# First projection weights split early, triangular inverses from two eight-row halves, one routing of all 1024 tokens

## The chip, the cores and the metric

The kernel runs on one core of a Trainium2 chip. The metric is the device time of one execution in microseconds (us). The core has five engines that work side by side from programs of their own: PE (TensorE, matrix products), DVE (VectorE), ACT (ScalarE), POOL (GpSimd) and SP (SyncE, which here only issues transfers). Each engine takes its instructions strictly in order; semaphores make it wait for other engines and for DMA transfers. SP and ACT each have a DMA queue of their own.

## The reference

1024 tokens of width 1024 in fp32 pass a first block (input projection, multiscale pool, RWKV7 mixing, output projection, LayerNorm, mixture of experts, LayerNorm) and then a second block of two attention layers with modulations from a conditioning vector. What the change touches is in the first block:

```python
def rwkv7_step(state, inp):
    r, decay, k, v, kk, a = inp
    sa = jnp.einsum('bhij,bhj->bhi', state, -kk)
    state = (state * decay[:, :, None, :]
             + sa[..., None] * (kk * a)[:, :, None, :]
             + v[..., None] * k[:, :, None, :])
    out = jnp.einsum('bhij,bhj->bhi', state, r)
...
    g_prob = jax.nn.softmax(hf @ router_group + router_group_b, axis=-1)
    g_top_p, g_idx = lax.top_k(g_prob, 1)
    e_sel = jnp.take_along_axis(e_logits, g_idx[:, :, None], axis=1)[:, 0]
    e_top_logit, e_idx = lax.top_k(e_sel, TOP_K)
    weights = g_top_p * jax.nn.softmax(e_top_logit, axis=-1)
...
    hid = jax.nn.silu(xb @ exp_gate[e]) * (xb @ exp_up[e])
    return (hid @ exp_down[e]) * wgt[:, None]
```

The scan over tokens is computed in chunks of 64: the steps of a chunk become products with the inverse of a unit lower triangular 64 x 64 matrix. The modulations ("mods") of the second block are 48 small products of the conditioning vector with 1024 x 128 weight blocks.

## The kernel before, in words

fp32 accuracy comes from splitting each operand into a high and a low fp32r part and adding three products (`mm3`, lines 104 to 106: hi·hi, lo·hi, hi·lo). A weight block is loaded (512 KB), its high part is copied by ACT (`wh`, line 460), and its low part is subtracted by POOL (`wl`, line 467).

Five stages follow each other in the trace: `phase_lowrank` (0 to 111 us), `phase_units` (to about 825), `phase_out` (to 939), `phase_moe` (to about 1260), the second block (to the end, untouched by the change).

- `phase_lowrank` projects the columns of the low-rank branches and makes decay and gates. A `Timeline` sets its order. Its tile pools are freed at its end, and the tiles of `phase_units` take that memory. Twelve memsets on POOL (lines 430 to 443) clear them, after the last transfers out of the old tiles.
- `phase_units` works on 12 units (6 head pairs x 2 halves of the sequence). The lanes of a unit (project, tokens, within, solve, inverse, chain, finish and so on) are generators; the table `PLAN` says at which slot each advances, relative to the unit's slot 24·v, and `ORDER` ranks lanes within a slot. So several units overlap, with a unit each 24 slots or some 48 us. `project` multiplies by three weight blocks j = 0, 1, 2 of 24 matmuls each, issues the load of a block two ahead, and splits the next one. The load is one of SP's, into a single buffer `w`.
- `solve` inverts, for 64 matrices at once (8 chunks x 2 heads x 4 diagonal blocks, one per partition), a 16 x 16 triangle, row by row on DVE: 15 steps of a product and a reduction. Then the result `Tn` goes out to DRAM (`tnd`) and comes back in eight loads to the block layout `T16`; `inverse` transposes it on DVE into `T16T` (line 745) and widens it to 64 x 64 by products.
- `chain` carries the state through the chunks of a unit. PE, ACT (`XB` and `R`, line 786) and DVE (`XA` and `R`, lines 784 and 807) hand each step on to one another.
- `mods` is a generator too; `MODP` gives the slots of its 96 pieces. A piece has eight matmuls (line 1723) on a 512 KB load from ACT's queue, then a copy on ACT, two selecting matmuls (line 1730) and a sum on DVE. After the 24th and 48th a transpose of the collected gates follows on PE (line 1741).
- `phase_out` makes the output projection, LayerNorm and router logits of the token tiles; `Route.part` picks groups and experts for tiles 0 to 3 in the middle and for 4 to 7 at the end, `slots` turns ranks into row numbers by products with one-hot matrices, and the expert weights are already loaded and partly split ("presplit", line 1431 on POOL). Then `phase_moe` gathers the tokens of each expert (indirect transfers from POOL) and runs 32 experts.

The 15 steps of `solve` before (lines 717 to 722) read:

```python
for t in range(1, 16):
    nc.vector.tensor_tensor(pr[:, :t, :t], Tn[:, 0:t, 0:t].rearrange("p s c -> p c s"),
                            LT[:, 0:t, t:t + 1].rearrange("p s o -> p o s").to_broadcast([64, t, t]), op=OP.mult)
    nc.vector.tensor_reduce(Tn[:, t, 0:t], pr[:, :t, :t], axis=AX.X, op=OP.add)
    yield
```

Of the kernel before, what the change touches and what calls it, by code (L numbers as in the profile page):

```python
# [129 lines left out]
def phase_mix(g):  # L130

    nc, tc, a = g.nc, g.tc, g.a
    c = ExitStack()
    with c:
        big = c.enter_context(tc.tile_pool(name="mxx", bufs=1, reuse_waits="tile"))
        xh, xl = (big.tile([P, KT, 512], F32R, name=n) for n in ("xh", "xl"))
        g.csil = big.tile([P, KT, 32], F32, name="csil")  # L140
        phase_lowrank(g, xh, xl)
        phase_units(g, [xh[:, k] for k in range(KT)], [xl[:, k] for k in range(KT)])


def phase_lowrank(g, xh0, xl0):

    nc, tc, a = g.nc, g.tc, g.a
    with ExitStack() as c:
        pool = lambda n, b, **k: c.enter_context(tc.tile_pool(name=n, bufs=b, reuse_waits="tile", **k))
        big, wp, zp, one = pool("pjx", 1), pool("pjw", 2), pool("pjy", 2), pool("pj1", 1)  # L150
# [47 lines left out]
        def w_load(col0):  # L198
            W[col0] = wp.tile([P, KT, P], F32, name="w")
# [171 lines left out]
XSTEP, PSTEP, PSTEP2, BOFF, BSTEP = 2.0, 0.9, 1.4, 8, 2.39  # L371
PAR1, PREP1 = 17.55, 18.1
# [12 lines left out]
    "solve": [-22, -22, -22, -22, -22, -20, -20, -20, -20, -20, -20, -19, -18, -18, -17, -17],  # L385
# [15 lines left out]
MODP = [-69] + [p + i for p in sorted([24 * u + d for u in range(-3, 8) for d in (8, 12, 17)] + [24 * u + 3 for u in range(-2, 9)]  # L401
                                     + [-27, -3, 21, 45]) for i in range(2)]
# [9 lines left out]
def phase_units(g, xh, xl):  # L412
    nc, tc, a = g.nc, g.tc, g.a
    with ExitStack() as c:
        wp = c.enter_context(tc.tile_pool(name="uw", bufs=2, reuse_waits="tile"))
# [28 lines left out]
        f = sm.tile([P, NU, HC], F32, name="f")  # L444
        mk = cv(g, "maskL").rearrange("p (o x t) -> p o x t", o=1, x=2)
        U = [Ctx() for _ in range(NU)]
        W = {}

        def wload(b):
            if b < 3 * NU:  # L450
                v, j = divmod(b, 3)
                col0 = 256 + (6 * j + v % NPAIR) * P
                W[b] = wp.tile([P, KT, P], F32, name="w" if b else "wm", bufs=1)
                nc.sync.dma_start(W[b], a["w_in"][0, :, col0:col0 + P].rearrange("(k p) c -> p k c", p=P))

        def wsplit(b):
            if b < 3 * NU:
                w = W[b]
                wh, wl = (wp.tile([P, KT, P], F32R, name=n) for n in ("wh", "wl"))
                nc.scalar.activation(wh, w, AF.Copy)  # L460
                W[b] = (wh, wl, w)

        def wsplit2(b):
            if b < 3 * NU:
                wh, wl, w = W[b]
                for c0 in range(0, KT, 2):
                    nc.gpsimd.tensor_tensor(wl[:, c0:c0 + 2], w[:, c0:c0 + 2], wh[:, c0:c0 + 2].bitcast(F32), op=OP.subtract)  # L467
# [93 lines left out]
        def tokens(v):  # L561
# [34 lines left out]
            fv = f[:, v, :, None]  # L596
# [116 lines left out]
        def solve(v):  # L713

            u = U[v]
            pr = sm.tile([64, 15, 15], F32, name="pr")
            LT = u.LT
            for t in range(1, 16):
                nc.vector.tensor_tensor(pr[:, :t, :t], Tn[:, 0:t, 0:t].rearrange("p s c -> p c s"),
                                        LT[:, 0:t, t:t + 1].rearrange("p s o -> p o s").to_broadcast([64, t, t]), op=OP.mult)  # L720
                nc.vector.tensor_reduce(Tn[:, t, 0:t], pr[:, :t, :t], axis=AX.X, op=OP.add)
                yield
            nc.sync.dma_start(g.tnd[v % 2], Tn.rearrange("p a b -> p (a b)"))
            d = g.tnd[v % 2]
            for hd in range(2):
                for b in range(4):
                    o = 64 * hd + 16 * b
# [282 lines left out]
def phase_out(g, hres, ex, early):  # L1010

    nc, tc, a = g.nc, g.tc, g.a
    with ExitStack() as c:
# [210 lines left out]
        for _ in r4:  # L1224
            pass
# [1916 lines left out]
```

## Time and profile before

| what | value |
|---|---|
| runs | 3299.97, 3303.45, 3313.67 us (median 3303.45) |
| profiled execution | 3299.23 us, span 3297.5 us |
| mean granted TensorE clock | 0.947 of full speed |
| PE busy | 2958.0 us (90%) |
| DVE busy | 2053.0 us (62%) |
| ACT busy | 1587.1 us (48%) |
| POOL busy | 1705.2 us (52%) |
| PE weight loads (beside the matmuls) | 2085.7 us (63%) |

The span runs from the first to the last instruction; the execution's own time adds 1.7 us around it. PE is the busiest engine, so the time is PE's work plus the gaps in it. A gap's releaser is the event that ended it. What an engine other than PE does matters where it ends such a gap.

### The profile page before, as it was taken

To read this page: it belongs to the slowest core of one execution; us is meant where nothing else is said; L and a number is where in the kernel's file an instruction comes from. 1 tells how busy PE (TensorE), PEld (TensorE's weight loads), DVE (VectorE), ACT (ScalarE), POOL (GpSimd) and SP (SyncE) were. 2 spreads that over 40 slices of the span, in tenths; PEclk is the share of its full clock that TensorE was granted. 3 is DMA by queue.
4 is the path that set the end of the run, shared out by engine and by line. 5 is a ranking of instruction groups with operands and counts; after the bars stand their busy time and mean duration, and the time that the engine had idled before them with its cause. 6 is when DMAs were issued, how large, how long until landed. Compare 5 with 4: busy or idle time off the path is not lost. (4 is left out here: it accounts for less than half of the span.)

```text
span 3297.5 us, 49255 instructions
## 1 busy us (share of the span) xinstructions
PE 2958.0 (90%) x17406; PEld 2085.7 (63%) x17406; DVE 2053.0 (62%) x3309; ACT 1587.1 (48%) x3058; POOL 1705.2 (52%) x1916
## 2 busy tenths in 40 slices
PE   7789899888779986899988898988998989999998
PEld 5466666656557655799845454467776756565556
DVE  2167677763679877775256675747257246666656
ACT  4345555553459876432144444545345235554442
POOL 0266667665435453643046565767356216464665
PEclk9789999988879998899999999999999989999999
DMA  5476776554889997423121111246134311111136
GB/s 201 148 180 164 197 179 154 146 159 132 274 280 320 325 333 249 144 81 107 57 65 49 45 50 39 79 145 224 37 103 154 112 49 63 47 45 39 45 107 219
DMA packets 430972, 457.26 MB, mean 139 GB/s; under 512 B 123336, under 2 KB 351171, under 8 KB 430595
## 3 DMA queue, kind: packets, MB, share of 16 engines
q1 hardware_dynamic: 366944, 400.95, 39.5%
q10 hardware_dynamic: 56162, 36.04, 3.6%
q0 software_dynamic: 7616, 17.09, 1.6%
q8 instruction: 138, 2.26, 0.3%
q14 instruction: 112, 0.91, 0.1%
HBM read 329.39 MB, written 101.11 MB: 131 GB/s over the span
## 5 line engine op out<-in xcount | busy, mean ns | idle before, releaser
L2107 ACT ACTIVATE p<-st 128x512 f32<-128x512 f32 (+1 forms) x672 | 377.7, 585 | 378.6 <-PE st L2105 309.1
L2026 DVE TENSOR_REDUCE mx<-s 128x1 f32<-128x1280 f32 x256 | 380.6, 1487 | 273.0 <-PE s L2025 273.0
L2119 POOL TENSOR_TENSOR acc<-acc,p 128x256 f32<-128x256 f32 x512 | 414.9, 842 | 70.6 <-ACT p L2107 69.2
L2128 PE MATMUL o<-p,V 128*64 128x512 f32 (+1 forms) x1344 | 319.8, 597 | 0.0
L1431 DVE TENSOR_TENSOR wl<-wr,wh 128x1024 fp32r<-128x1024 f32 x156 | 228.1, 1490 | 41.6 <-ACT wh L1430 41.5
L2119 DVE TENSOR_TENSOR acc<-acc,p 128x512 f32<-128x512 f32 x256 | 228.3, 892 | 13.6 <-ACT p L2107 6.7
L104 PE MATMUL pz<-xh,wh 128*128 128x512 f32 x440 | 219.7, 499 | 2.1 <-ACT wh L460 2.1
L1430 ACT ACTIVATE wh<-wr 128x1024 fp32r<-128x1024 f32 x192 | 198.9, 1055 | 40.2 <-DMA wr<-in_exp_up_dram 19.4
L106 PE MATMUL pz<-xh,wl 128*128 128x512 f32 x440 | 180.1, 409 | 15.0 <-POOL wl L467 13.6
L105 PE MATMUL pz<-xl,wh 128*128 128x512 f32 x440 | 180.7, 411 | 0.0
L2144 POOL TENSOR_TENSOR rg<-rg,gt 128x256 f32<-128x256 f32 x72 | 64.5, 895 | 214.7 <-ACT rg L2141 213.5
L2119 POOL TENSOR_TENSOR acc<-p 128x256 f32<-128x256 f32 x72 | 53.6, 762 | 227.9 <-ACT p L2107 223.7
L2128 PEld LDWEIGHTS o<-p,V 128*64 128x64 f32 x1344 | 82.0, 136 | 140.4 <-issue 136.3
L104 PE MATMUL pj<-hh,wh 128*128 128x512 f32 (+1 forms) x416 | 160.8, 387 | 9.2 <-DVE xk L2782 4.6
L1789 POOL TENSOR_TENSOR wl<-wr,wh 128x512 fp32r<-128x512 f32 (+1 forms) x70 | 88.5, 1276 | 151.9 <-ACT wh L1787 151.6
L1431 POOL TENSOR_TENSOR wl<-wr,wh 128x1024 fp32r<-128x1024 f32 x36 | 89.1, 2477 | 146.5 <-ACT wh L1430 131.0
L106 PE MATMUL pj<-hh,wl 128*128 128x512 f32 (+1 forms) x416 | 156.4, 376 | 0.5 <-POOL wl L1789 0.5
L105 PE MATMUL pj<-hl,wh 128*128 128x512 f32 (+1 forms) x416 | 156.2, 376 | 0.0
L2105 PE MATMUL st<-QQ,K 128*128 128x512 f32 (+1 forms) x352 | 149.9, 427 | 4.5 <-ACT p L2107 4.3
L467 POOL TENSOR_TENSOR wl<-w,wh 128x256 fp32r<-128x256 f32 x140 | 110.5, 820 | 78.2 <-ACT wh L460 64.6
L106 PE MATMUL pj<-wh,hl 128*128 128x256 f32 x480 | 141.1, 294 | 4.6 <-POOL hl L1870 4.5
L105 PE MATMUL pj<-wl,hh 128*128 128x256 f32 x480 | 140.4, 293 | 4.7 <-DVE wl L1789 4.7
(524 smaller groups left out, 8457.4 us busy)
## 6 DMA issues: line engine op xcount, KB each, us to landing
wr<-in_exp_gate_dram SPq DMA_DIRECT2D x64, 512.0 KB
wr<-in_exp_up_dram SPq DMA_DIRECT2D x64, 512.0 KB
wr<-in_exp_down_dram SPq DMA_DIRECT2D x32, 1024.0 KB
w<-in_l_w_out_dram SPq DMA_DIRECT2D x56, 512.0 KB
wm<-in_l_w_mod_dram ACTq DMA_DIRECT2D x48, 512.0 KB
w<-in_w_in_dram SPq DMA_DIRECT2D x39, 512.0 KB
wr<-in_l_w_in_dram SPq DMA_DIRECT2D x33, 512.0 KB
y<-ysd SPq DMA_DIRECT2D x16, 512.0 KB
```

The source lines that it names most:

```text
L104: nc.tensor.matmul(out, lh, rh, start=start, stop=False)
L105: nc.tensor.matmul(out, lh, rl, start=False, stop=False)
L106: nc.tensor.matmul(out, ll, rh, start=False, stop=stop)
L467: nc.gpsimd.tensor_tensor(wl[:, c0:c0 + 2], w[:, c0:c0 + 2], wh[:, c0:c0 + 2].bitcast(F32), op=OP.subtract)
L1430: nc.scalar.activation(wh, w, AF.Copy)
L1431: eng.tensor_tensor(wl, w, wh.bitcast(F32), op=OP.subtract)
L1789: eng.tensor_tensor(st["l"][:, ks], st["w"][:, ks], st["h"][:, ks].bitcast(F32), op=OP.subtract)
L2026: nc.vector.tensor_reduce(m[:, j:j + 1], ps.rearrange("p a b -> p (a b)")[:, :SK], axis=AX.X, op=OP.max)
L2105: nc.tensor.matmul(st[:, :n], kk[:, kt * P:(kt + 1) * P], qv[:, pt.q0:pt.q0 + n], start=(j == 0), stop=(j == len(passes) - 1))
L2107: nc.scalar.activation(p[:, :n], st[:, :n], AF.Exp, scale=self.scale)
L2119: (nc.gpsimd if e == 1 else nc.vector).tensor_tensor(a, r.p[r.kts[0], e][:, cs] if r.first else a, r.p[r.kts[i], e][:, cs], op=OP.add)
L2128: nc.tensor.matmul(pt.po[64 * e:64 * e + 64, :n], pt.out["V"](e, kt), r.p[kt, e][:, :n], start=(r.first and i == 0), stop=(r.last and i == ...
```

## The change

Four parts. (1) The functions that load and split the unit projection's weights move into a class whose pool is opened ahead of `phase_lowrank`; block 0 is loaded and split and block 1 loaded inside `phase_lowrank` (`FIRSTW`), and the weight tiles no longer lie in memory that this stage frees. (2) `MODP` puts six fewer mods ahead of slot 0 and five instead of four into each of the units 0 to 7; the transposes after mods 24 and 48 come with the next piece. (3) `solve` inverts both 8 x 8 diagonal halves of each 16 x 16 triangle in the same 7 steps, and makes the lower left quarter from two products of 512 elements with their reductions. ACT copies a transposed `Tn` into `LT`, a second DRAM tile `ttd` and eight more loads fill `T16T`, and the two DVE transposes per unit go. (4) All eight token tiles are routed at once at the end of `phase_out`; the five presplit pieces on POOL go, and five pieces come to DVE at the end of the routing and after the first gather.

```diff
+        w = Weights(g, wp)
+        phase_lowrank(g, xh, xl, wp, w)
+        phase_units(g, [xh[:, k] for k in range(KT)], [xl[:, k] for k in range(KT)], wp, w)
...
+        for dt, f, b in FIRSTW:
+            at(ts[3] + dt, f, first, b)
...
+FIRSTW = (-12, Weights.load, 0), (4, Weights.load, 1), (8, Weights.split, 0), (10, Weights.split2, 0)
...
-    "solve": [-22, -22, -22, -22, -22, -20, -20, -20, -20, -20, -20, -19, -18, -18, -17, -17],
+    "solve": [-22, -21, -21, -20, -20, -19, -19, -18, -18, -17, -16],
...
-MODP = [-69] + [p + i for p in sorted([24 * u + d for u in range(-3, 8) for d in (8, 12, 17)] + [24 * u + 3 for u in range(-2, 9)]
-                                     + [-27, -3, 21, 45]) for i in range(2)]
+MODP = [-69] + [p + i for p in [-64, -55, -45, -36, -27, -16, -7] + [24 * u + d for u in range(8) for d in (3, 8, 12, 17, 21)] + [195]
+                for i in range(2)]
...
-            for t in range(1, 16):
...
+            for t in range(1, 8):
+
+                x = pr[:, 0:2, 0:t, 0:t]
+                nc.vector.tensor_tensor(x, h8(Tn, [[B, 2], [1, t], [16, t]]),
+                                        h8(LT[:, 0:1, t:t + 1], [[B, 2], [0, t], [16, t]]), op=OP.mult)
+                nc.vector.tensor_reduce(h8(Tn[:, t:t + 1, 0:1], [[B, 2], [1, t]]), x, axis=AX.X, op=OP.add)
                 yield
...
+            nc.vector.tensor_tensor(pr, h8(LT[:, 0:1, 8:9], [[1, 8], [0, 8], [16, 8]]),
+                                    h8(Tn, [[0, 8], [1, 8], [16, 8]]), op=OP.mult)
+            yield
+            nc.vector.tensor_reduce(m8, pr, axis=AX.X, op=OP.add)
+            yield
+            nc.vector.tensor_tensor(pr, h8(Tn[:, 8:9, 8:9], [[16, 8], [0, 8], [1, 8]]),
+                                    h8(m8, [[0, 8], [1, 8], [8, 8]]), op=OP.mult)
+            yield
+            nc.vector.tensor_reduce(Tn[:, 8:16, 0:8], pr, axis=AX.X, op=OP.add)
+            nc.scalar.activation(Tt, Tn.rearrange("p t c -> p c t"), AF.Copy)
+            for x, T, d in ((0, Tn, g.tnd[v % 2]), (1, Tt, g.ttd[v % 2])):
+                nc.sync.dma_start(d, T.rearrange("p a b -> p (a b)"))
+            for x, d in ((0, g.tnd[v % 2]), (1, g.ttd[v % 2])):
+                for hd in range(2):
+                    for b in range(4):
+                        o = 64 * hd + 16 * b
+                        dst = T16T[o:o + 16, :, hd, 16 * b:16 * b + 16] if x else T16[o:o + 16, :, 16 * b:16 * b + 16]
+                        nc.sync.dma_start(dst, bass.AP(
+                            tensor=d.tensor, offset=d.offset + (2 * b + hd) * 2048, ap=[[16, 16], [256, 8], [1, 16]]))
...
-            for e, sl in enumerate((lo, hi)):
-                nc.vector.transpose(T16T[sl, :, e, :], T16[sl])
...
-    "presplit": [40.1, 40.15, 40.2, 40.25, 43.6],
...
-    "route": [37, 38, 39, 40, 41, 42, 43, 44, 45],
...
+        def route():
+
             pr = pt.tile([P, 512], F32, name="pr")
+            for i, _ in enumerate(rt.part(0, 8, pr[:, 0:256].rearrange("p (i e) -> p i e", e=NE))):
+                if i == 4:
+                    shift(7, v, 0, 2)
+                    nc.scalar.dma_start(g.hd[7 * P:8 * P, :], hres[7])
+            slots(g, rt.rp, pr[:CAP, 256:320])
+            slot_rows(g, g.idx.rearrange("p q e -> p (q e)"), pr[:CAP, 256:320])
+            for _ in range(3):
+                ex.next(v, 0)
...
-        for _ in route(4, 8):
-            pass
+        route()
...
+        yield
         if n == 23:
...
-        yield
```

Where instructions move, three places matter. First PE at the end of `phase_lowrank`. `pz` is the accumulator of j = 0 (832 before, 829 now), `wh` and `wl` its weights; the rows of `zl`, `lw` and `lg` are the stage's own last products. Before:

```order
L284 MATMUL pA_725<-lg_135,gu_133 128x512
L104 MATMUL pz_832<-xh_107,wh_825 128x512
L105 MATMUL pz_832<-xl_108,wh_825 128x512
L335 MATMUL pA_730<-zl_721,pw1_213 128x512
L284 MATMUL pA_761<-lg_135,gu_133 128x512
L106 MATMUL pz_832<-xh_107,wl_826 128x512
L104 MATMUL pz_832<-xh_107,wh_825 128x512
```

Now (865 is the accumulator of j = 1):

```order
L313 MATMUL pA_738<-lg_137,gu_135 128x512
L104 MATMUL pz_829<-xh_109,wh_629 128x512
L105 MATMUL pz_829<-xl_110,wh_629 128x512
L106 MATMUL pz_829<-xh_109,wl_630 128x512
L104 MATMUL pz_865<-xh_109,wh_842 128x512
L105 MATMUL pz_865<-xl_110,wh_842 128x512
L364 MATMUL pA_743<-zl_734,pw1_215 128x512
L313 MATMUL pA_774<-lg_137,gu_135 128x512
L106 MATMUL pz_865<-xh_109,wl_843 128x512
```

All 24 products of j = 0 now stand ahead of the stage's last eight, and what stands behind those is j = 1.

Second, POOL at the same place: the subtraction for block 0 and the memsets. `T`, `L`, `H`, `Tn`, `Sc` are tiles of `phase_units`. Before:

```order
L430 MEMSET T_796 128x512
L435 MEMSET L_798 128x1024
L440 MEMSET Tn 64x16
L443 MEMSET Sc 128x384
L467 TENSOR_TENSOR wl<-wm,wh 128x256 x4
L467 TENSOR_TENSOR wl<-w,wh 128x256 x12
```

Now:

```order
L171 TENSOR_TENSOR wl<-wm,wh 128x256 x4
L461 MEMSET T_805 128x512
L466 MEMSET L_807 128x1024
L471 MEMSET Tn 64x16
L474 MEMSET Sc 128x384
L171 TENSOR_TENSOR wl<-w,wh 128x256 x12
```

Block 0's four subtractions pass the memsets; those of block 1 stay behind them.

Third, SP's queue around the load of a weight block that follows a solve (`T_796` and `T_805` are `T16`; `XA`, `XB` belong to the chain, `mix` to the unit's output). Before:

```order
L454 DMA w<-in_w_in_dram 128x8x128
L705 DMA XA<-vt 64x4x64 x4
L705 DMA XB<-vt 64x4x64 x4
L723 DMA tnd_96<-Tn 64x256
L728 DMA T_796<-tnd_96 16x8x16 x8
L454 DMA w<-in_w_in_dram 128x8x128
```

Now:

```order
L158 DMA w<-in_w_in_dram 128x8x128
L716 DMA XA<-vt 64x4x64 x4
L716 DMA XB<-vt 64x4x64 x4
L753 DMA tnd_97<-Tn 64x256
L753 DMA ttd_99<-LT 64x256
L759 DMA T_805<-tnd_97 16x8x16 x8
L759 DMA T16T<-ttd_99 16x8x16 x8
L158 DMA w<-in_w_in_dram 128x8x128
```

A write and eight loads more stand ahead of the same weight load.

## Rows read from the trace of the kernel before

**Rows 1.** The windows view by stage. Columns: start:end, us, busy us (instructions) per engine, PEclk, DMA share, GB/s.

```profile
111.00:155.00 44.00, 26.59 (x129) 20.16 (x130) 2.31 (x8) 6.93 (x12) 19.39 (x29) 0.69 0.40 128
...
235.00:825.00 590.00, 535.06 (x5522) 377.13 (x5522) 412.62 (x1106) 303.73 (x676) 382.79 (x537) 0.95 0.62 162
...
939.00:1260.00 321.00, 301.95 (x1452) 208.10 (x1451) 275.18 (x312) 259.10 (x347) 164.94 (x93) 0.98 1.02 327
```

**Rows 2.** The timeline of PE, 94 to 235. Columns: start us, busy us, instruction, [idle before <-releaser].

```profile
103.17 3.37 PE L335 MATMUL pA<-zl,pw 128*128 128x512 f32 x4 [4.30 <-issue]
...
124.33 0.80 PE L106 MATMUL pz<-xh,wl 128*128 128x512 f32 x1 [13.57 <-POOL wl L467]
...
147.53 1.08 PE L1723 MATMUL pA<-wm,csil 128*32 128x128 f32 x16 [1.53 <-DMA wm<-in_l_w_mod_dram]
...
155.78 0.66 PE L575 MATMUL pA<-const,z 128*128 128x128 f32 x4 [0.19 <-DVE z L526]
...
214.83 2.76 PE L652 MATMUL pA<-G,BK 64*128 64x128 f32 x16 [5.10 <-DVE BK L619]
```

**Rows 3.** The timeline of POOL, 110 to 150, same columns.

```profile
116.11 1.84 POOL L435 MEMSET L<- 128x1024 f32 x2 [2.32 <-DMA gtp<-gt]
...
123.56 2.77 POOL L467 TENSOR_TENSOR wl<-wm,wh 128x256 fp32r<-128x256 f32 x4
```

**Rows 4.** The timeline of ACT's DMA queue, 95 to 150, same columns.

```profile
143.68 0.37 ACTq L1710 DMA_DIRECT2D wm<-in_l_w_mod_dram  x1
```

**Rows 5.** The waits of PE from 235 to 780: us in total, times, longest us.

```profile
PE cA L793 <- DVE XA L807: 17.4, 27, 4.9
...
PE pA L1741 <- DVE gcol L1735: 5.6, 2, 2.8
...
PE cB L805 <- ACT XB L786: 5.3, 6, 2.4
```

**Rows 6.** The lines of DVE from 160 to 780: busy us, mean ns | idle before, releaser.

```profile
L719 DVE TENSOR_TENSOR pr<-Tn,LT 64x1 f32<-64x1 f32 (+4 forms) x180 | 88.1, 489 | 11.4 <-DMA LT<-labd 7.2
...
L721 DVE TENSOR_REDUCE Tn<-pr 64x1 f32<-64x1 f32 (+4 forms) x180 | 41.6, 231 | 6.2
...
L745 DVE STREAM_TRANSPOSE T16T<-T 64x512 f32<-64x512 f32 x24 | 16.9, 705 | 0.4
...
L771 DVE TENSOR_TENSOR T<-pA,T32T 64x512 f32<-64x512 f32 x22 | 15.0, 683 | 1.1 <-PE pA L750 0.7
```

**Rows 7.** The timeline of SP's DMA queue, 496 to 520, columns as in rows 2.

```profile
500.51 0.49 SPq L723 DMA_DIRECT2D tnd<-Tn  x1
...
504.40 3.65 SPq L728 DMA_DIRECT2D T<-tnd  x8
...
508.46 0.39 SPq L454 DMA_DIRECT2D w<-in_w_in_dram  x1
```

**Rows 8.** The timelines of ACT and, last row, PE at two weight splits.

```profile
403.02 1.06 ACT L460 ACTIVATE wh<-w 128x1024 fp32r<-128x1024 f32 x1 [1.39 <-DMA w<-in_w_in_dram]
...
514.63 1.06 ACT L460 ACTIVATE wh<-w 128x1024 fp32r<-128x1024 f32 x1 [0.26 <-DMA w<-in_w_in_dram]
...
404.37 0.27 PE L805 MATMUL cB<-XB,TK 128*64 128x64 f32 x1 [2.43 <-ACT XB L786]
```

**Rows 9.** The timelines of PE (first three) and DVE at the routing, 900 to 950.

```profile
912.24 1.89 PE L1140 MATMUL pl<-rw,ht 128*128 128x36 f32 x8 [11.76 <-DVE lgt L1146]
...
933.12 0.44 PE L1294 MATMUL pr<-both,trir 128*128 128x128 f32 x1 [6.92 <-DVE both L1287]
...
944.10 1.51 PE L1490 MATMUL pt<-const,xg 96*128 96x96 f32 x8 [3.97 <-DMA xg<-hd,idx]
...
902.37 2.29 DVE L1277 TENSOR_TENSOR t<-t,sel 128x32 f32<-128x32 f32 x1
...
930.70 0.19 DVE L1277 TENSOR_TENSOR t<-t,sel 128x32 f32<-128x32 f32 x1
```

**Rows 10.** The waits of ACT from 1120 to 1260, columns as in rows 5.

```profile
ACT wh L1430 <- DMA wr<-in_exp_up_dram: 18.0, 11, 3.6
```

More of the change, by code (lines that the diff above doesn't have):

```diff
@@ L139, in phase_mix, with __init__, load, split @@
         xh, xl = (big.tile([P, KT, 512], F32R, name=n) for n in ("xh", "xl"))
[L140 to L145, printed above, removed]
+        g.csil = big.tile([P, KT + 16, 2], F32, name="csil")
+        wp = c.enter_context(tc.tile_pool(name="uw", bufs=2, reuse_waits="tile"))
+        w = Weights(g, wp)
+        phase_lowrank(g, xh, xl, wp, w)
+        phase_units(g, [xh[:, k] for k in range(KT)], [xl[:, k] for k in range(KT)], wp, w)
+class Weights:
+    def __init__(self, g, wp):
+        self.g, self.wp, self.W = g, wp, {}
+    def load(self, b):
+        if b < 3 * NU:
+            v, j = divmod(b, 3)
+            col0 = 256 + (6 * j + v % NPAIR) * P
+            self.W[b] = self.wp.tile([P, KT, P], F32, name="w" if b else "wm", bufs=1)
+            self.g.nc.sync.dma_start(self.W[b], self.g.a["w_in"][0, :, col0:col0 + P].rearrange("(k p) c -> p k c", p=P))
+    def split(self, b):
+        if b < 3 * NU:
+            w = self.W[b]
+            wh, wl = (self.wp.tile([P, KT, P], F32R, name=n) for n in ("wh", "wl"))
+            self.g.nc.scalar.activation(wh, w, AF.Copy)
+            self.W[b] = (wh, wl, w)
+    def split2(self, b):
+        if b < 3 * NU:
+            wh, wl, w = self.W[b]
+            for c0 in range(0, KT, 2):
+                self.g.nc.gpsimd.tensor_tensor(wl[:, c0:c0 + 2], w[:, c0:c0 + 2], wh[:, c0:c0 + 2].bitcast(F32), op=OP.subtract)
+def phase_lowrank(g, xh0, xl0, wp, first):
     nc, tc, a = g.nc, g.tc, g.a
@@ L443, in phase_units @@
         nc.gpsimd.memset(Sc, 0.0)
-        f = sm.tile([P, NU, HC], F32, name="f")
         mk = cv(g, "maskL").rearrange("p (o x t) -> p o x t", o=1, x=2)
         U = [Ctx() for _ in range(NU)]
[L447 to L467, printed above, removed]
+        W, wload, wsplit, wsplit2 = weights.W, weights.load, weights.split, weights.split2
         O = {}
@@ L1205, in phase_out @@
             at(t, early)
-        r4 = route(0, 4)
-        for t in OUT["route"]:
-            at(t, lambda: next(r4, None))
         at(40, lambda: (cw.close(), ex.open()))
@@ L1212, in phase_out @@
                       (0.4, lambda: turn(7, 0)), (0.5, lambda: turn(7, 1)), (0.6, lambda: keep(7, 0)), (0.7, lambda: keep(7, 1)),
[L1213 to L1215 removed]
+                      (0.8, lambda: gain(7, e, 0, 2)), (0.9, lambda: logits(7, 0)), (1.0, lambda: logits(7, 1)),
+                      (1.4, lambda: logit_b(7))):
             at(t + dt, f)
[L1217 to L1218 removed]
         for t in OUT["again"]:
@@ L1321, in weights, with slots, slot_rows @@
         v.tensor_tensor(g.w12[:, 1], g.w12[:, 0], d, op=OP.mult)
-def slots(g, pool, pt, i0, i1, name="slotA"):
+def slots(g, pool, pt, name="slotA", bufs=2):
     nc = g.nc
-    A = pool.tile([P, 2, i1 - i0, CAP], F32R, name=name)
     for j in range(2):
-        nc.vector.tensor_tensor(A[:, j], cv(g, "iota")[:, None, :CAP].to_broadcast([P, i1 - i0, CAP]),
-                                g.rank[:, j, i0:i1, None].to_broadcast([P, i1 - i0, CAP]), op=OP.is_equal)
-    yield
-    for i in range(i0, i1):
-        for j in range(2):
-            nc.tensor.matmul(pt, A[:, j, i - i0], g.tokv[:, j, i].rearrange("p q e -> p (q e)"), start=(i == i0 and j == 0), stop=(i == i1 - 1 and j == 1))
-def slot_rows(g, idx, pt, rows, first):
-    if first:
-        return g.nc.vector.tensor_scalar(rows, pt, 2048.0, None, op0=OP.add)
-    else:
-        return g.nc.vector.tensor_tensor(idx.rearrange("p q e -> p (q e)"), pt, rows, op=OP.add)
+        for i0 in (0, 4):
+            A = pool.tile([P, 4, CAP], F32R, name=name, bufs=bufs)
+            nc.vector.tensor_tensor(A, cv(g, "iota")[:, None, :CAP].to_broadcast([P, 4, CAP]),
+                                    g.rank[:, j, i0:i0 + 4, None].to_broadcast([P, 4, CAP]), op=OP.is_equal)
+            for i in range(4):
+                nc.tensor.matmul(pt, A[:, i], g.tokv[:, j, i0 + i].rearrange("p q e -> p (q e)"),
+                                 start=(j + i0 + i == 0), stop=(j == 1 and i0 + i == 7))
+def slot_rows(g, rows, pt):
+    return g.nc.vector.tensor_scalar(rows, pt, 2048.0, None, op0=OP.add)
 DE = 256
```

73 lines of the change are left out of this document (25 added, 48 removed).

## The prediction, as it went on record

> **What bounds the kernel now.** I read the busy shares of the page first, then the windows by stage, then in each stage that the change touches the timeline of PE with the idle time ahead of each instruction, and last the queues of the engines that end those gaps. PE is busy 90% of the span, and in the unit stage 535 of 590 us [rows 1]: whatever is taken off another engine counts only as far as that engine ends a gap of PE.
>
> Four places hold such gaps. At the start of the units PE is busy 26.6 of 44 us, at a granted clock of 0.69 [rows 1]: it stands 13.57 us for a weight's low part from POOL, and POOL made it at 123.56, as soon as its memsets were through, which in turn waited for transfers out of the old tiles [rows 2, 3]. Through the units DVE ends the largest group of gaps, 17.4 us in 27 waits, beside 5.6 us in two waits of a transpose for the sum just ahead of it [rows 5]. ACT ends 5.3 us [rows 5]. At the routing PE waits 11.76 us for logits that DVE adds behind a routing whose operations on 32 elements last 2.29 us, where the same operation lasts 0.19 us later [rows 9]. In the experts' stage the transfers are full all the time (share 1.02, 327 GB/s), and late in it ACT waits 18.0 us for arriving weights [rows 1, 10].
>
> **The start of the units (12 us gained).** Block 0 is split ahead of the memsets, and all 24 products of j = 0 stand ahead of the low-rank stage's last products. There PE idled 4.30 us [rows 2]; 22 products more at the window's mean of 26.59/129 = 0.21 us are 4.5 us, so they fit into that idle. The 13.57 us stay: j = 1 now waits for the same memsets and for the subtraction behind them, in the very place where j = 0 stood. What is gained is the time of one of three blocks. They fill, with three mods, the stretch from 124.33 to 155.78 [rows 2]: a third of 31.5 us is 10.5. Six mods leave the stage before slot 0. Their products return one per later unit and so gain nothing, but a mod at the start comes before its load has landed (1.53 us of idle at 147.53 [rows 2], 3.85 us after the issue at 143.68 [rows 4]); I count that once: 10.5 + 1.5 = 12. Upper bound: that wait for all six, 10.5 + 9.2 = 19.7. Lower bound: 2, if the chain of unit 0 sets the pace, since PE there waited 5.10 us for DVE's `BK` [rows 2].
>
> **The two transposes after the mods (5 us).** They now come with the next piece, when the sum has long been made. 5.6 us [rows 5] go; each transpose may meet another small wait, so I take 5, between 0 and 5.6.
>
> **The inverse (6 us).** Before, a unit costs DVE (88.1 + 41.6 + 16.9)/12 = 12.2 us [rows 6]. After, 7 steps of a product and a reduction at 0.49 + 0.23 make 5.0 us; two products and two reductions of 512 elements at the 0.68 us of line 771 [rows 6] make 2.7, in all 7.8. The reduction of 512 has no row of its own; that of line 721 lies below it and the product is the nearest of that size. So DVE saves 4.4 us per unit and 53 us in all. This is not PE's time. Of PE's 17.4 us of waiting behind line 807 [rows 5] I give back a third, 6: the rest follows the chain's own round trip, whose sums wait for PE. Bounds 0 and 17.4. ACT's new copy of 64 x 256 is smaller than the weight copy of 1.06 us [rows 8], so at most 1 us per unit; ACT is busy 304 of 590 us [rows 1], which hides it unless the last reduction is late: behind the copy, in ACT's order, stand the chain's `XB` and `R`.
>
> **The transfers of the inverse (11 us lost).** SP issues in order. Before, `tnd` goes out at 500.51, the eight loads at 504.40 for 3.65 us, then at 508.46 the weight load [rows 7], whose data ACT splits at 514.63 after having waited 0.26 us for them [rows 8]: so that load is just in time. Now a write and eight more loads stand ahead of it. At 3.65 us for eight, the weight load leaves 3.65 us later; where the last reduction, which moves behind `G` and one slot back, also delays the first write, up to 1.65 us more, 5.3 in all. Landing took 514.37 - 508.46 = 5.9 us with another 512 KB block on the way from ACT's queue; one block alone took 3.85 us [rows 4], and 3.65 us later that other block is through. So the data come 3.65 + 3.85 - 5.9 = 1.6 us late by the one price and 5.3 us late by the sum of the others. ACT stands meanwhile, and behind its split stand the chain's copies. That this reaches PE, the trace shows at 403.02: ACT waited 1.39 us for such a load, and PE then 2.43 us for `XB` [rows 8]. Nine solves have a weight load behind them; at the first two the chain isn't running yet. 7 x 1.6 = 11. Bounds 0 (the next gap of ACT takes it) and 9 x 5.3 = 48.
>
> The Trainium skill (DMA: Bandwidth & Descriptors, "Rules for kernel authors") advises to join small transfers, because below 64 KB one pays mostly overhead, and gives about 2.0 us fixed per transfer under "Anatomy of one DMA"; that speaks against eight more loads of 8 KB. Paid one after the other that would be an estimated 16 us ahead of each weight load, and the sum would come out slower by a hundred. The trace differs for SP's queue: eight were issued in 3.65 us, 0.46 us each [rows 7], so the fixed part overlaps, and I use the row.
>
> **The routing (4 us).** The first half's routing leaves the middle, and with it PE's 11.76 us wait for the logits [rows 9]. The routing at the end handles eight tiles instead of four: some twenty operations that grow by a third of 0.19 us [rows 9], an estimate of 1.3 us. The first gathered tokens would reach PE, instead of at 944.10 [rows 9], 10.5 us earlier. But expert weights move at 327 GB/s all through the next stage [rows 1], and ACT waits for them later [rows 10]. The five early split pieces on POOL freed load buffers; without them I count 12 instead of 14 loads of 1 MB begun before the first gather, and two loads at 1.05 MB / 327 GB/s = 3.2 us give 6.4 back. 10.5 - 6.4 = 4. Bounds -6 (nothing gained, all given back) and 11.8.
>
> **The sum.** 12 + 5 + 6 + 4 - 11 = 16 us less than the profiled execution's 3299.23: 3283. The median of the runs is 4.2 us above that execution, the fastest run 0.7 above; I keep near the execution and say **3284**.
>
> **Rivals.**
> - *The weight load takes back more than all the rest (slower).* Place: SP's queue behind `T16T`, then ACT's split, then PE's chain. If every one of the nine loads comes 5.3 us late, 48 us go; the relief of DVE is then worth nothing, since ACT ends the gaps, and 12 + 5 + 4 = 21 remain: 27 slower, 3326. It decides from about 4.2 us of PE per load: 9 x 4.2 = 38 is 17 more than the 21 that remain. For: 0.26 us of slack, and 1.39 us turned into 2.43 [rows 8]. Against: the load lands faster alone [rows 4], and a queue that is late may still find a later, slower unit. Chance 0.18.
> - *The start gives nothing.* The round trip of unit 0 through DVE, POOL and ACT replaces the memsets, as at 214.83 [rows 2]: 2 instead of 12, so 3293. For: PE's work before slot 0 thins out by six mods. Against: PE is busy nearly without a break from 155.78 to that wait, so it has had work to move up. Chance 0.15.
> - *The routing's gain is lost to the transfers.* If the experts' stage is bound by its loads from end to end, an earlier start gains nothing and the two loads cost 6.4: 3283 + 10 = 3293. For: share 1.02 [rows 1]. Against: loads waited for are 18.0 us late in the stage [rows 10], while PE is busy 302 of 321 us [rows 1]. Chance 0.12.
> - *The change doesn't free DVE where it ends gaps.* Then 6 us less, 3289, inside the forecast's own spread.
>
> **How the numbers follow.** A measurement of this kernel can tell about 0.5%, 16.5 us, from no change: faster is below 3287, slower above 3320. The forecast has 0.55, of which 0.47 lie below 3287 and 0.08 above, as its sum stands only 3 us from that bound. With 0.15 and 0.12 for the two rivals at 3293, no change has 0.35; slower has 0.18. The terms' spreads upward of the gain are 8, 11, 8 and, for the weight loads, 11 us, together some 20 to 24: low end **3260**. The other end goes to **3320**: it takes in both rivals at 3293 and a weight load that costs 37 us more than I take, and leaves out the worst of the first rival.
>
> **What would show it.** In the changed profile PE should run the whole of j = 0 before 111 us and still wait some 13 us for `wl`, and unit 0's transposes should start near 144 instead of 155.78. No wait for `gcol` should be left. DVE's time per inverse should be near 7.8 us. In ACT's waits, the one for `w` in the unit stage should grow from a few us to some 15; if it grows to 40 and PE's wait for `XB` with it, the first rival holds. PE's first product on gathered tokens should stand some 10 us less after the last unit than now, and ACT's waits for expert weights grow. I am wrong if `w` costs nothing (then the time is near 3272) or if the start's gap only moves to another releaser.

## The result, and the profile after

The changed kernel took 3337.95 us, the median of 8 runs from 3327.39 to 3347.64, against 3306.93 for the kernel before: a ratio of 1.0073, 95% interval 1.0052 to 1.0094. It is slower by 0.7%, where 3284 and a range up to 3320 were forecast. The profiled execution took 3329.10 us, its span 3327.3 us.

The windows by stage, against [rows 1], with the same columns:

```profile
111.00:155.00 44.00, 29.42 (x147) 22.23 (x148) 4.23 (x10) 12.88 (x19) 20.82 (x31) 0.77 0.38 114
...
235.00:825.00 590.00, 509.75 (x5261) 361.66 (x5261) 348.31 (x887) 286.26 (x638) 358.62 (x494) 0.89 0.64 159
...
939.00:1260.00 321.00, 291.37 (x1384) 202.53 (x1385) 271.18 (x336) 245.76 (x328) 158.05 (x89) 0.94 1.00 323
```

At the start the same 44 us hold more PE work. In the unit stage the same 590 us hold less: 5261 matmul records instead of 5522, at a mean granted clock of 0.89 instead of 0.95. The timeline of PE, against [rows 2, 9] (rows of the units' start, of the routing and of the first gathered tokens):

```profile
122.76 0.80 PE L106 MATMUL pz<-xh,wl 128*128 128x512 f32 x1 [14.03 <-POOL wl L171]
...
144.81 0.60 PE L585 MATMUL pA<-const,z 128*128 128x128 f32 x4
...
953.18 0.55 PE L1306 MATMUL pr<-both,trir 128*128 128x256 f32 x1 [7.04 <-DVE both L1304]
...
965.97 1.52 PE L1504 MATMUL pt<-const,xg 96*128 96x96 f32 x8 [3.70 <-DMA xg<-hd,idx]
```

The wait for the low part is still there (14.03 us), and unit 0's transposes start at 144.81 instead of 155.78. The transposes of the next two units start at 178.65 and 222.45, where they stood at 191.62 and 235.82: 13.0 and 13.4 us earlier. From then on the lead melts. The sixth and tenth units' transposes start at 384.35 and 609.63, against 380.68 and 577.35, and the last state of the chain is written at 854.38 instead of 816.60. So between the third unit and the end of the chain 51 us are lost. After that the changed kernel is faster again: from the last state to the first gathered tokens it takes 111.6 us instead of 127.5, and from there to the last expert's output 333.0 instead of 326.8 (1298.98 - 965.97, and 1270.86 - 944.10). The second block takes the same time in both, within 2 us.

What PE waits for from 220 to 790, against [rows 5]:

```profile
PE cB L833 <- ACT XB L814: 38.8, 19, 5.1
...
PE cA L821 <- DVE XA L835: 1.0, 2, 0.6
...
PE pA L1757 <- DVE gcol L1750: 0.3, 1, 0.3
```

The wait behind DVE's state update (line 835, line 807 before) has gone from 17.4 to 1.0 us, and the wait for `gcol` from 5.6 to 0.3. In their place PE waits 38.8 us for ACT's chain copy `XB`, where it was 5.3. What ACT waits for from 140 to 800:

```profile
ACT wh L164 <- DMA w<-in_w_in_dram: 41.4, 13, 4.8
...
ACT LT L751 <- DVE Tn L750: 30.0, 11, 3.2
```

These two stand ahead of the chain copies in ACT's order. Before, in the same stretch:

```profile
ACT wh L460 <- DMA w<-in_w_in_dram: 3.3, 5, 1.4
```

One unit shows how it comes about. SP's queue, against [rows 7]:

```profile
520.01 0.49 SPq L753 DMA_DIRECT2D tnd<-Tn  x1
520.68 0.49 SPq L753 DMA_DIRECT2D ttd<-LT  x1
523.40 3.66 SPq L759 DMA_DIRECT2D T<-tnd  x8
527.17 4.61 SPq L759 DMA_DIRECT2D T16T<-ttd  x8
531.87 0.40 SPq L158 DMA_DIRECT2D w<-in_w_in_dram  x1
```

From the write of `tnd` to the issue of the weight load pass 11.86 us, where it was 7.95. On the mean of the nine solves with a weight load behind them these are 12.1 us (10.8 to 13.5) and 7.0 (5.8 to 8.0). ACT in the same unit, against [rows 8], at the transposing copy and at the weight split:

```profile
520.02 0.64 ACT L751 ACTIVATE LT<-Tn 64x256 f32<-64x256 f32 x1 [3.22 <-DVE Tn L750]
...
535.94 1.06 ACT L164 ACTIVATE wh<-w 128x1024 fp32r<-128x1024 f32 x1 [3.40 <-DMA w<-in_w_in_dram]
```

And PE's next product of the chain:

```profile
537.29 0.37 PE L833 MATMUL cB<-XB,TK 128*64 128x64 f32 x1 [2.78 <-ACT XB L814]
```

ACT came to the split at 532.54 and stood 3.40 us; PE stood 2.78 us for `XB`, which ACT makes right behind the split. What the granted clock did around this stall, in windows of 4 us, with the columns of [rows 1]:

```profile
532.00:536.00 4.00, 2.51 (x31) 1.48 (x30) 1.18 (x3) 0.57 (x3) 3.02 (x4) 1.00 0.72 203
536.00:540.00 4.00, 2.71 (x42) 2.18 (x42) 0.52 (x2) 2.06 (x5) 2.78 (x4) 0.61 0.73 225
540.00:544.00 4.00, 4.00 (x20) 2.91 (x18) 0.65 (x3) 0.69 (x3) 0.62 (x1) 0.50 0.75 196
544.00:548.00 4.00, 4.00 (x56) 3.30 (x59) 2.11 (x6) 0.44 (x2) 0.00 (x0) 0.61 0.64 125
```

PE is busy for 5.2 of the 8 us from 532 to 540, and then works on at a granted clock of 0.50, the lower of its two levels (1.2 GHz), from 540 to 544, and at 0.61 on the mean of the four microseconds on either side.

What the inverse costs PE over all units can be read beside the fourth run below, the changed kernel with the inverse of before. The windows reach from the transposes of the first unit to those of the twelfth, first the changed kernel, then that run, with the columns of [rows 1]:

```profile
144.81:714.28 569.47, 496.61 (x5013) 357.39 (x5011) 335.50 (x830) 281.06 (x598) 348.59 (x469) 0.90 0.65 158
```

```profile
142.79:679.03 536.24, 480.62 (x5013) 344.27 (x5013) 375.57 (x971) 274.65 (x588) 345.20 (x470) 0.96 0.67 165
```

Both hold 5013 matmul records. Of the 33.2 us between them 16.0 are busy time, the same products at a lower granted clock (0.90 instead of 0.96), and 17.2 are idle time of PE.

### The profile page after: what moved, and what is told of

Same layout as the page of the kernel before. It is cut to its first block, busy times and chain, and to the rows that moved or that the text cites. A ratio compares the mean times of both kernels' runs of the same rounds, so it can differ in the third digit from the quotient of the medians.

```text
span 3327.3 us, 49266 instructions
## 1 busy us (share of the span) xinstructions
PE 2979.2 (90%) x17402; PEld 2101.9 (63%) x17402; DVE 1996.1 (60%) x3111; ACT 1596.5 (48%) x3070; POOL 1705.0 (51%) x1912
## 5 line engine op out<-in xcount | busy, mean ns | idle before, releaser
L1445 DVE TENSOR_TENSOR wl<-wr,wh 128x1024 fp32r<-128x1024 f32 x161 | 235.4, 1488 | 42.4 <-ACT wh L1444 42.3
L171 POOL TENSOR_TENSOR wl<-w,wh 128x256 fp32r<-128x256 f32 x140 | 111.6, 828 | 87.7 <-ACT wh L164 84.0
L1445 POOL TENSOR_TENSOR wl<-wr,wh 128x1024 fp32r<-128x1024 f32 x31 | 77.1, 2487 | 138.9 <-ACT wh L1444 98.6
```

The costliest lines, as they stand in the source:

```text
L171: self.g.nc.gpsimd.tensor_tensor(wl[:, c0:c0 + 2], w[:, c0:c0 + 2], wh[:, c0:c0 + 2].bitcast(F32), op=OP.subtract)
L1445: eng.tensor_tensor(wl, w, wh.bitcast(F32), op=OP.subtract)
```

## The experiments

Three theories were held against each other. Theory 1: the eight further loads on SP's queue make the weight load late, and ACT's in-order wait for it stops the chain. Theory 2: ACT's transposing copy, which stands behind DVE's last reduction, stops it. Theory 3: something else in the change, such as the fifth modulation per unit. Ratios are of the kernel run to the kernel before on the same chip, with 95% intervals. The twelve runs were taken in three groups of four on three chips, where the kernel before took 3297.02, 3298.94 and 3315.85 us; across groups, and with the changed kernel, which no group holds, only ratios are compared.

**The further loads behind the weight load.** The eight loads become a lane of their own, last in the order of slot -15.

```diff
+    "t_load": [-15],
...
-            for x, d in ((0, g.tnd[v % 2]), (1, g.ttd[v % 2])):
...
+        def t_load(v):
+            d = g.ttd[v % 2]
+            for hd in range(2):
+                for b in range(4):
+                    o = 64 * hd + 16 * b
+                    nc.sync.dma_start(T16T[o:o + 16, :, hd, 16 * b:16 * b + 16], bass.AP(
+                        tensor=d.tensor, offset=d.offset + (2 * b + hd) * 2048, ap=[[16, 16], [256, 8], [1, 16]]))
```

> The changed kernel, with the eight loads of T16T put behind the weight load on SP's queue; the write of ttd and ACT's transposing copy stay where they are. Theory 1 (the weight load, 4 us late at nine solves, stops ACT and so the chain): the wait for w in ACT shrinks from 41 us to under 10, a unit takes about 49 instead of 54.5 us, and the time falls by some 40 to about 3295. Theory 2 (ACT stands at the transposing copy, 30 us in 11 waits, behind DVE's last reduction): that wait stays, and the time falls by less than 10, to about 3330. Theory 3 (neither; the slots of the solve or the fifth modulation per unit do it): no change, 3338.

Measured: 1.0023 (1.0011 to 1.0035), so half a per cent or some 16 us back of 24. ACT's waits:

```profile
ACT LT L752 <- DVE Tn L751: 32.4, 12, 3.5
...
ACT wh L164 <- DMA w<-in_w_in_dram: 12.7, 7, 2.9
```

The wait for `w` fell from 41.4 to 12.7 us, and the copy's wait stayed. The gain is 16 of the 40 us that theory 1 expected, and more than the 10 that theory 2 allows.

**Copy and further loads behind the weight load.**

```diff
-            nc.scalar.activation(Tt, Tn.rearrange("p t c -> p c t"), AF.Copy)
...
         def t_load(v):
+            nc.scalar.activation(U[v].LT, Tn.rearrange("p t c -> p c t"), AF.Copy)
+            nc.sync.dma_start(g.ttd[v % 2], U[v].LT.rearrange("p a b -> p (a b)"))
```

> As the run before, with the transposing copy and the write of ttd behind the weight load too, so that ACT waits at neither. Theory 1: about as fast as the run before, 3285 to 3295. Theory 2: 3295 to 3305, and clearly faster than the run before (by 25 or more). Both together: 3280. Theory 3: 3338.

Measured: 1.0051 (1.0031 to 1.0070), slower than the run before; all three theories missed. The copy's wait is gone, but:

```profile
ACT wh L164 <- DMA w<-in_w_in_dram: 19.5, 6, 5.3
```

The largest of these waits are at other weight loads than the ones behind a solve (5.3 us at 381, 4.9 at 403, 3.6 at 555), and PE waits 21.7 us for `XB`, where it was 15.4 in the first run. A wait that the changed kernel doesn't have comes in addition:

```profile
PE pA L786 <- DMA T16T<-ttd: 3.7, 2, 1.9
```

The later `T16T` now reaches PE by itself. That SP, busy longer with `T16T`, comes late to the loads of the next slots as well would explain the other waits; no run tests it.

**The copy on DVE.**

```diff
-            nc.scalar.activation(Tt, Tn.rearrange("p t c -> p c t"), AF.Copy)
+            nc.vector.tensor_copy(Tt, Tn.rearrange("p t c -> p c t"))
```

> The changed kernel, with the transposing copy on DVE right behind the last reduction instead of on ACT; transfers as changed, so that the weight load stays late. Theory 1: less than 10 faster, 3328 to 3338, ACT's wait for w stays at 35 to 45 us. Theory 2: the 30 us of waiting go, time near 3300. Theory 3: 3338 or a little more, for DVE's added work.

Measured: 1.0120 (1.0101 to 1.0140), slower than the change itself by its ratio (1.0073), where theory 2 wanted some 30 us less. The sizes of theory 1 (no slower than the change, 35 to 45 us of wait) are missed as well, though that the loss stays without ACT's copy is its sign. ACT's wait for `w` has grown:

```profile
ACT wh L164 <- DMA w<-in_w_in_dram: 50.0, 14, 6.6
```

**The inverse of before in the changed kernel** (the edit is the diff of `solve`, its slots and the two transposes, backwards).

> The changed kernel with the inverse of before: its 15 steps, slots, transposes on DVE and eight loads; early weights, the slots of the modulations and the single routing stay as changed. Theories 1 and 2: the unit period goes back to about 48 us and what the other three parts gained stays (13 us at the start of the units, some 5 at the transposes of the modulations, 8 at the routing and the experts): about 3280. Theory 3 with the fifth modulation per unit as the cause: 3320 or more.

Measured: 0.9969 (0.9954 to 0.9983), some 10 us faster than before. So the inverse costs 1.0073 - 0.9969 = 1.04%, 34 us (26 to 43 by the two intervals), and the other three parts are not the cause of the loss: theory 3 falls. They gain 10 us, less than half of the 26 expected here. ACT's wait for `w`:

```profile
ACT wh L164 <- DMA w<-in_w_in_dram: 7.6, 4, 4.7
```

**Weight loads from ACT's queue.**

```diff
-            self.g.nc.sync.dma_start(self.W[b], self.g.a["w_in"][0, :, col0:col0 + P].rearrange("(k p) c -> p k c", p=P))
+            (self.g.nc.sync if b < 3 else self.g.nc.scalar).dma_start(self.W[b], self.g.a["w_in"][0, :, col0:col0 + P].rearrange("(k p) c -> p k c", p=P))
```

> The changed kernel, with the unit projection's weight loads (from the fourth on) issued from ACT's DMA queue instead of SP's, so that nothing of the inverse stands ahead of them; the transposing copy stays. Theory 1 (SP's queue carries more than it can, and every weight load in it comes late): ACT's wait for w goes below 8 us, and the time falls to 10 to 20 us below the one with T16T behind the load, some 0.2% below before. Theory 2 (ACT stands at the transposing copy): only some 15 us below the changed kernel, since the copy's 30 us stay. If a weight load now waits on ACT for its buffer, ACT's own order suffers: 0.5% or more above before.

Measured: 1.0010 (0.9993 to 1.0027), 0.63% or 21 us below the changed kernel:

```profile
ACT LT L751 <- DVE Tn L750: 31.6, 12, 3.2
...
ACT wh L164 <- DMA w<-in_w_in_dram: 8.3, 5, 2.9
```

The same transfers stand on SP, the copy waits as long as it did, and yet 21 of the inverse's 34 us are gone, with the wait for `w`. So the place of the weight load in that queue costs this much. The time lies between what theory 1 expected (some 0.998) and theory 2 (some 1.0028), so this run alone doesn't decide on the rest.

**Both: loads from ACT's queue and the later copy.** The edits of the second and the fifth run together.

> As the run before, with the transposing copy, the write of ttd and the loads of T16T a slot later, so that ACT waits neither for a late weight load nor for DVE's last reduction. Theories 1 and 2 together: the inverse then costs nothing and DVE's relief shows: 0.5 to 0.8% below before, below the kernel with the old inverse (0.3% below before). If it stays above that one, the late T16T or SP's other transfers hold the units up.

Measured: 1.0034 (1.0020 to 1.0048). Not faster than without the later copy, as in the second run, and far from the 0.992 to 0.995 expected. The expectation names the late `T16T` for this case, and the second run's trace shows it at PE; how much of the time it is stays open.

**Old inverse and old slots of the modulations.** `MODP` of before in the kernel of the fourth run.

> The kernel with the old inverse and, further, the slots of the modulations of before (13 pieces ahead of slot 0, four per unit); early weights, the transposes with the next piece and the single routing stay. If the six moved modulations only return what they saved, as forecast: within 4 us of the kernel with the old inverse. If five per unit cost more (their loads come too late, a wait of 1 us each in seven units beside their products): some 5 to 10 us faster at the units' end, of which the start takes 5 back.

Measured: 0.9965 (0.9951 to 0.9979), the same as with the new slots. Here unit 0's transposes start at 148.26, and a unit takes 47.9 us (475.81 to 571.51 in two). In the fourth run they start at 142.79 and a unit takes 49.6 (475.88 to 624.53 in three). So what the moved modulations save at the start, 5.5 us, they give back in the units: 1.7 in each of these, and 8.6 from the first unit's transposes to the twelfth's (536.24 and 527.67). Six units hold one more than before; units 0 and 1 had five already.

**The kernel before with eight loads more.** Nothing of the change is in this one.

```diff
-            for hd in range(2):
+            for hd in (0, 1, 0, 1):
```

> The kernel before with the eight loads of T16 issued twice after each solve, the second eight with the same data; nothing else differs, so that only SP's queue ahead of the weight load grows, by 3.7 us. Theory 1: the weight load comes late nine times by 1.5 to 4 us, each costs PE 2 to 5 us, 20 to 40 in all: 0.6 to 1.2% above before. Theory 2: under 0.2%.

Measured: 1.0159 (1.0142 to 1.0176), 52 us above before, more than theory 1 expected. SP's queue in one unit:

```profile
535.16 0.49 SPq L723 DMA_DIRECT2D tnd<-Tn  x1
...
538.96 11.17 SPq L728 DMA_DIRECT2D T<-tnd  x16
...
550.25 0.40 SPq L454 DMA_DIRECT2D w<-in_w_in_dram  x1
```

From the first of the sixteen loads to the end of the last pass 11.17 us, where it was 3.65 for eight, and the weight load came 15.1 us behind the write of `tnd`. A single issue took no longer than before, where the eight took 0.33 to 0.44 us (shortest, median and longest, in ns):

```profile
L728 SPq DMA_DIRECT2D T<-tnd x16: 303/428/430, 539.0 to 549.7; - x16
```

The rest is a pause of 3.9 us ahead of the thirteenth load. SP's waits at these loads name a modulation's weight load on ACT's queue (before, 4.1 us in four waits):

```profile
SPq L728 <- DMA wm<-in_l_w_mod_dram: 32.5, 12, 5.6
```

So the edit delays the weight load by more than the issue time of eight loads: by 7.2 us on the mean of the nine solves, where the changed kernel delays it by 5.1. What ACT then waited for, and PE:

```profile
ACT wh L460 <- DMA w<-in_w_in_dram: 47.6, 11, 6.9
```

```profile
PE cB L805 <- ACT XB L786: 35.6, 12, 6.6
```

The chain of the changed kernel, reproduced by repeated transfers alone: the weight load late, ACT standing 4.3 us each time, PE standing 3.0 us for `XB`; PE's waits for the later `T16` itself are 4.1 us in all. Together with the fifth run, which takes only the weight load out of that queue, this shows theory 1.

**Halves, but `T16T` by DVE.** The two DVE transposes come back in `inverse`; the copy, the write of `ttd` and the further loads go.

> The changed kernel with the inverse from two halves, but T16T made on DVE by the two transposes of before: no transposing copy on ACT, no write of ttd, no further loads on SP. Theory 1 (the further transfers on SP) and theory 2 (the copy) both expect the loss gone: 0.3% to 0.6% below before, at or below the kernel with the old inverse (0.31% below), since DVE still saves some 3 us per unit. If it stays above that, the later last reduction (a slot later, in front of the weight load) is itself a cost: ACT's wait for w then is 10 us or more.

Measured: 0.9979 (0.9961 to 0.9998), the loss is gone, though the gain is below the 0.3% to 0.6% expected. ACT's wait for `w`:

```profile
ACT wh L164 <- DMA w<-in_w_in_dram: 10.2, 6, 3.8
```

The halves themselves cost nothing that shows, and gain nothing that shows, beside the old inverse's 0.9969. The 10.2 us are what the expectation gave as the sign of a last reduction that comes too late; the next run tries that.

**Earlier slots for it.**

```diff
-    "solve": [-22, -21, -21, -20, -20, -19, -19, -18, -18, -17, -16],
+    "solve": [-22, -22, -22, -21, -20, -20, -20, -19, -18, -18, -17],
```

> As the run before, with the inverse's eleven pieces from slot -22 to -17, as before, instead of -22 to -16. If the last reduction's place matters for the weight load behind it: 3 to 8 us faster than the run before and ACT's wait for w under 5 us. If not: the same within 3 us.

Measured: 0.9999 (0.9974 to 1.0024), no gain: nothing shows that the last reduction's place matters. The wait for `w` stayed at 10.0 us, and a new one came up on PE:

```profile
PE pA L663 <- POOL BK L629: 11.0, 7, 1.8
```

**The same with the old slots of the modulations.**

> As the run before, with the modulations' slots of before, as a candidate for the fastest: with the old inverse these slots made no difference that could be measured (0.35% against 0.31% below before), so the same within 5 us; 0.4% to 0.7% below before.

Measured: 0.9972 (0.9943 to 1.0001), a smaller gain than expected and not told apart from the two before it. The lowest ratios of this study are those of the two kernels with the old inverse, 0.9969 and 0.9965; this run and the ninth aren't told apart from them.

**An idle copy.** The ninth kernel with ACT's transposing copy put back; nothing reads what it writes.

```diff
+            nc.scalar.activation(Tt, Tn.rearrange("p t c -> p c t"), AF.Copy)
```

> As the first run of these four, with ACT's transposing copy put back behind the last reduction, though nothing reads what it writes: the price of that wait alone. Theory 2: ACT stands some 30 us at it, and the time rises by 10 to 30 us against the first run. Theory 1 alone: by less than 5 us.

Measured: 0.9986 (0.9970 to 1.0001), 0.07% above the ninth, which took 3305.74 us on the same chip where this one took 3308.38; by the two intervals the copy's wait costs at most some 10 us. ACT's waits:

```profile
ACT LT L751 <- DVE Tn L750: 27.8, 10, 3.2
...
ACT wh L164 <- DMA w<-in_w_in_dram: 14.0, 4, 6.2
```

ACT stands 27.8 us at the copy and the time hardly moves. So theory 2, with its 10 to 30 us, falls as the cause of the loss.

## Why the prediction was wrong, point by point

**The transfers of the inverse: the step that failed.** Place and order were named: SP's queue, ACT's split, PE's `XB`. What failed is the price of a late weight load, 7 x 1.6 = 11 us. With 6 us of relief on DVE the inverse was to cost 5 us; by the fourth run it costs 34. That is 29 of the 40 us between the 16 forecast as a gain and the 24 measured as a loss (0.73%); the other three parts, with 10 us instead of 21, are the remaining 11. Term by term:

- *How late the load is issued.* I took 3.65 us for the eight loads alone and kept the rest for the bound. The trace has both: 3.9 us between `tnd` and the load, and `tnd` itself some 1.3 us later against ACT (12.5 instead of 13.9 us ahead of the split). In the queue rows 5.2 of the bound's 5.3 us are found, and this unit is one of the mild ones: over the nine solves the way from `tnd` to the load grew by 5.1 us on the mean.
- *How fast it lands.* That was right for this unit: issued at 531.87 and used at 535.94, 4.1 us against the 3.85 taken, so that 5.2 - 1.8 = 3.4 remain, which is the wait that ACT shows. One reading was wrong: the 0.26 us of [rows 8] are no slack, as the first rival has it. ACT came at 514.37 and stood until 514.63, so the load was already 0.26 us late.
- *How often.* Not in seven places but at all nine solves: ACT's waits there are 1.75 to 4.84 us, 32.6 in all.
- *What a late load costs PE.* I counted ACT's wait and nothing else. From the first unit's transposes to the twelfth's the inverse adds 17.2 us of idle time and 16.0 us for the same products at the lower granted clock. For this second half the sum had no term.

In the middle of the stage a unit took 54.6 us (500.36 to 609.63, two units), 49.4 with the old inverse (475.88 to 574.69) and 47.8 before (481.74 to 577.35). So 5.2 of the 6.8 us are the inverse's and 1.6 the fifth modulation's. In the kernel before with repeated loads, which has no fifth modulation, a unit takes the same 54.6 us (516.37 to 680.23, three units), with a load that is later still.

The wait of 1.39 us in [rows 8] was no warning of the clock's share. The unit around it is long in other kernels too: 53.4 us before (380.68 to 434.06), 56.7 in the fourth run, 55.2 in the seventh. Before, the lower clock in it follows another stall of PE, and behind the 2.43 us for `XB` at 404.37 the clock stayed up:

```profile
391.15 0.34 PE L798 MATMUL cA<-R,T 128*64 128x64 f32 x1 [4.52 <-DVE R L784]
```

```profile
392.00:396.00 4.00, 4.00 (x17) 3.28 (x18) 3.63 (x13) 1.63 (x4) 3.14 (x4) 0.50 0.80 162
...
404.00:408.00 4.00, 3.63 (x43) 2.68 (x44) 3.09 (x9) 2.09 (x7) 3.83 (x4) 1.00 0.31 59
```

**The first rival** (0.18, at 3326, 27 slower) is what came, with the sign that the prediction gave for it: 41.4 us of ACT's wait for `w`, and PE's wait for `XB` with it. That its number fits within 3 us is luck in part: it put the loads at 48 us and the other three parts at 21, where 34 and 10 were measured.

**What argued against the rival** didn't hold: a load that lands alone is faster, but by 1.8 us of 5.2, and a slower unit didn't give the next load more room, since the chain of `tnd`, loads and split moves along with it: at the last four solves ACT still waits 4.32, 3.40, 3.81 and 3.96 us.

**The start of the units** was right in its sum and its mechanism: 11.0 us at the first unit and 13.4 at the third, against 12, and the wait for `wl` stayed (14.03). Its two terms were off in opposite ways, which is luck: the block j = 0 by itself moved unit 0 by 7.5 us (148.26 against 155.78 in the seventh run), where a third of the stretch, 10.5, had been taken, and the moved modulations by 5.5, where 1.5 had been. **The transposes after the modulations** were right in the changed kernel: 0.3 instead of 5.6 us are left. In the fourth run one of the two waits stayed, with 2.8 us. **The modulations' return** was put at nothing beside 1.5 us at the start. In the time it is nothing (0.9965 and 0.9969), but only as the 8.6 us that it costs the units stand against the 5.5 saved at the start.

**The inverse on DVE** was right in size and wrong in effect. The lines of DVE in the changed kernel, against [rows 6]:

```profile
L738 DVE TENSOR_TENSOR pr<-Tn,LT 64x2 f32<-64x2 f32 (+6 forms) x84 | 33.1, 394 | 10.4 <-DMA LT<-labd 9.0
...
L747 DVE TENSOR_TENSOR pr<-Tn,LT 64x512 f32<-64x512 f32 x12 | 18.9, 1578 | 0.0
...
L740 DVE TENSOR_REDUCE Tn<-pr 64x2 f32<-64x2 f32 (+6 forms) x84 | 15.8, 188 | 2.9
...
L742 DVE TENSOR_TENSOR pr<-LT,Tn 64x512 f32<-64x512 f32 x12 | 12.7, 1058 | 0.0
...
L745 DVE TENSOR_REDUCE LT<-pr 64x64 f32<-64x512 f32 x12 | 8.1, 678 | 0.4
...
L750 DVE TENSOR_REDUCE Tn<-pr 64x64 f32<-64x512 f32 x12 | 8.0, 668 | 0.0
```

They sum to 96.6 us, 8.05 per unit, against 7.8 forecast and 12.2 before, though single terms were off: the second product takes 1.58 us where I took 0.68. The 6 us for PE didn't come: with the transfers gone, halves and old inverse can't be told apart (0.9979 and 0.9969). What PE waits for from 220 to 790 shows why, with the old inverse (fourth run) and with the halves (ninth):

```profile
PE cA L804 <- DVE XA L818: 18.7, 31, 4.8
...
PE cB L816 <- ACT XB L797: 3.8, 4, 2.0
```

```profile
PE cB L833 <- ACT XB L814: 14.5, 12, 3.5
...
PE cA L821 <- DVE XA L835: 9.4, 16, 3.8
```

Half of the wait for DVE goes, and the wait for ACT's `XB` takes its place. The rival that DVE's relief doesn't reach PE is borne out within those intervals.

**The routing** was put at 4 us and gave 9.7 in the profiled executions: 15.9 earlier at the first gathered tokens (10.5 forecast) and 6.2 given back in the experts' stage (6.4 forecast). That the two loads are what was given back isn't shown: ACT's waits for expert weights, which were to grow, are 34.3 us from the first gathered tokens to the end of the stage, against 32.8 before. The rival that all of it is lost to the transfers didn't come.

**The three parts together** were to give 12 + 5 + 4 = 21 us and gave about 10 by the ratio of the fourth run. The lead of 13 us at the start of its units is gone by their end, since the fifth modulation costs each unit 1.7 us and not the 1.0 of its products: PE waits 7.5 us for its loads in seven places there.

**Open** is why about 0.3% (0.9979 against 1.0010, on two chips) remains when the weight loads leave SP's queue for ACT's, and how much of the loss with the later copy is the late `T16T`. In the fifth run PE waits longer than in the ninth for the modulations' loads (12.2 us, 6.3), which now share a queue with the weight loads, and for `XB` (18.1, 14.5). That other transfers on SP come late as well would explain both, too. Neither was tried.

## What to carry to other kernels

Price a transfer added to an in-order queue by what stands behind it: here 3.7 us of issue time and the waits that came with it, ahead of a load that was already 0.26 us late, made the inverse 34 us dearer, while the work it took off DVE gained nothing that could be measured. Count what a stall does to PE beyond the wait: half of the loss in the units was the same products at a lower clock. Compare a long unit with the same unit of other kernels before its length is put down to one wait in it. A long wait of an engine is no price either: 27.8 us at the idle copy cost next to nothing, 41 us at the weight split went with the loss.

## What the runs showed of the hardware that was not expected

After the stall PE worked on at the lower granted clock: 0.50 from 540 to 544, although it was busy without a break there. After a stall of 2.43 us in the kernel before it stayed at 1.00; what makes the difference no run shows. Issuing a load of 128 pieces of 64 bytes took SP 0.30 to 0.44 us, with sixteen in a row as with eight. But in the kernel with sixteen SP also stood at such loads, 5.6 us at the longest, for a transfer of ACT's queue: the thirteenth of the sixteen waits on the completion semaphore (111) that the modulation's load issued by ACT at 543.39 counts up, and went out at 548.41. The advice of the Trainium skill (DMA: Bandwidth & Descriptors, "Rules for kernel authors") to join small transfers agrees with the outcome. The 2.0 us each that the prediction quotes from that page, where they are fitted to transfers issued from GpSimd, isn't what these loads cost SP; their price came from the order in the queue. And of three DVE products of 512 elements on 64 partitions, the one that reads `pA` took 0.68 us, the two that read `LT`, `Tn` and broadcast patterns 1.06 and 1.58.
